# Four of a pair's seven block products in one PSUM bank

## The chip, the core and the metric

The kernel runs on one core of a Trainium2 chip. The metric is the time of one execution on the device, in microseconds. Its engines work side by side, each through its own instructions in order: TensorE (PE in the profile, its weight loads PEld), VectorE (DVE), ScalarE (ACT), GpSimd (POOL), and SyncE (SP), which here only issues transfers. TensorE writes its results to PSUM, eight banks of 128 x 512 float32 each; VectorE and ScalarE read them from there.

## The reference

The kernel computes one encoder block over 1024 tokens of width 1024: three attention mixers side by side, and a gate for each of them and each channel. What matters for this change are the gates. `mg` is the last part of one large projection of the normalised input, and gives 3 x 1024 gate channels per token:

```
h = rms_norm(x, g_pre)
..., mg = split(h @ w_in)
gates = sigmoid(mg + b_merge)            # 3 branches x 1024 channels
merged = gates[0] * ya + gates[1] * yb + gates[2] * ym
out = merged @ w_out
x = x + rms_norm(out, g_post)
```

Everything is float32. The kernel splits each operand of a product into a rounded high part and a remainder (low part) and adds three products: high x high, high x low, low x high.

## The kernel before, in words

The 24 groups of 128 gate channels are its units of work here. Two are computed elsewhere; the other 22 form 11 pairs. A pair's result is a matrix of 2 x 128 gate channels by 1024 tokens, over an inner width of 1024. The kernel computes it by Strassen's scheme in Winograd's form: weights and tokens are cut into 2 x 2 blocks, and seven block products take the place of eight. Each block product is 128 x 512 over an inner width of 512, twelve matmuls of 128 x 512 (four slices, three terms each). The token blocks (`TB`: B11, B21, B22 and the sums T1 to T4) are made once. The weight blocks are A11, A12 and A22 of a pair and its sums S1 to S4, listed with their partners in `PRODUCTS` (L1780).

The stage has its own PSUM pool with six banks (`phase_psum("ps_w", s1=6)`, L1767). The scheduler is off in it: TensorE, ScalarE, VectorE, GpSimd and SyncE each carry out their instructions in the order in which the program text issues them. The loop at L1937 goes over pairs `n` and products `i`, and does three things each time:

- `prod(n, i)` (L1801) issues the twelve matmuls of product `i` into a new bank.
- `evac(...)` (L1822) reads the product *before* this one out of its bank. A11 is copied to `p1` by ScalarE. A12 is added to `p1` by VectorE, multiplied with the row `rb` and returned to ScalarE as a gate result. S2 is added to `p1` into `v`, S3 to `v` into `y`, S4 to `v` into `w`, all by VectorE. A22 is added to `y`, S1 to `y` and to `w`; these give the other gate results. Each gate result is one addition, one multiplication (L1817, L1818), one tanh on ScalarE (L1819) and a 256 KB store from ScalarE's queue (L1820).
- `slot(n, i)` (L1882) prepares what comes later. `block_of` (L1791) splits a block: its high part by ScalarE (L105), its low part by VectorE (L106), into one of five buffers `ch`. `weight_sum` (L1786) makes S1 to S4 of the next pair on GpSimd (L1789), S2 from S1 and S4 from S2. `own_blocks` (L1697) splits A11 and A12 of the next pair at once. `load_pair` (L1693) loads 512 KB of weights on SyncE's queue; two buffers `wr` serve all pairs, so the second load of pair n+1 waits until A22, the last block taken from pair n's second load, has been split. The slots also carry other work: the last item of one attention mixer in pairs 0 to 5 (`com`: loads, weightings by VectorE at L1677, additions by GpSimd at L1679), and loads and gate products (`g_load`, `g_mult`, L1857) of the next stage in pairs 6 to 9.

What a slot hands back (`then`: tanh and store) is issued after the slot's work. In the last pair the order of products differs (`nth`, L1797): A22 comes before S4 and S1, and S1 goes to the other bank pool (`psd`), since the next stage opens a new pool over the six banks. That stage (`y_unit`, L1985) begins with products of the token tiles `hh` and `hl`; `g_split` (L1859) writes their new contents, the lower halves in slots 3 and 4 of the last pair, the upper halves, which hold T4 until A22 is done, in slots 5 and 6.

Of the kernel before, what the change touches and what calls it, by code (L numbers as in the profile page):

```python
# [10 lines left out]
AF = mybir.ActivationFunctionType  # L11
OP = mybir.AluOpType
# [38 lines left out]
def block(ctx: ExitStack, tc: tile.TileContext, x, xT, memT, cst, msk, bcst, tabA, gpost,  # L51
          wu, wv, wb, wmem, wbr, wout, out):
    nc = tc.nc
    V, A, G, PE = nc.vector, nc.scalar, nc.gpsimd, nc.tensor
# [7 lines left out]
    def psd():  # L62
        return ps.tile([P, 512], F32, name="d", tag="d", bufs=2)
# [15 lines left out]
    def pss1():  # L79
        return bank["p"].tile([P, 512], F32, name="s1", tag="s1", bufs=bank["n"][1])  # L80
# [16 lines left out]
    rb = const.tile([P, S], F32, name="rb")  # L97
# [6 lines left out]
    def split(dst_h, dst_l, src):  # L104
        A.activation(dst_h, src, AF.Copy)  # L105
        V.tensor_tensor(dst_l, src, dst_h.bitcast(F32), op=OP.subtract)  # L106
# [15 lines left out]
    def passes(out_ps, terms):  # L122
        n = len(terms)
        for i, (a, b) in enumerate(terms):
            PE.matmul(out_ps, a, b, start=i == 0, stop=i == n - 1)  # L125
# [119 lines left out]
    def pool(name, side="left"):  # L245
        p = tc.tile_pool(name=name, bufs=1, side=side, reuse_waits="tile")
        return p, p.__enter__()

    def close(p):
        p.__exit__(None, None, None)  # L250
# [209 lines left out]
    for k in range(8):  # L460
        if k % 2 == 0:
            load_wkv(k // 2)
        for e in range(2 if k == 0 else 1):
            t = slice(e * 512, e * 512 + 512) if k == 0 else slice(0, S)
# [29 lines left out]
    for c in range(2):  # L494
        t = st.tile([P, 4, 256], F32, name=f"mt{c}", tag=f"xk{c}")
# [215 lines left out]
    half = [slice(0, 512), slice(512, 1024)]  # L711
# [183 lines left out]
    lo, hi = half  # L895
    PRODUCTS = (("A11", "B11"), ("A12", "B21"), ("S2", "T2"), ("S3", "T3"), ("S4", "B22"), ("S1", "T1"), ("A22", "T4"))
# [6 lines left out]
    def slot():  # L903
        return vp.tile([P, 1024], R, name="sl", bufs=2)
# [264 lines left out]
    for n in range(28):  # L1169
        i, k = divmod(n, 4)  # L1170
# [17 lines left out]
        for stage in (2, 1, 0):  # L1188
            r, at = divmod(n - 6 - (0, 2, 3)[stage], 3)
# [26 lines left out]
    for n in range(28):  # L1216
        i, k = divmod(n, 4)
        an, bn = PRODUCTS[i]
# [4 lines left out]
        for j in range(4):  # L1223
            c = slice(j * 128, j * 128 + 128)
            for q, (a, b) in enumerate(((bh[:, c], wh_[:, k]), (bl[:, c], wh_[:, k]), (bh[:, c], wl_[:, k]))):
                PE.matmul(now[j // 2][:, half_cols[j % 2]], a, b, start=k == 0 and j % 2 == 0 and q == 0,  # L1226
                          stop=k == 3 and j % 2 == 1 and q == 2)
# [23 lines left out]
    for n in range(6):  # L1251
        for i, (an, bn) in enumerate(PRODUCTS):
            dst = pss1()
            ah, al = [z.rearrange("p (k f) -> p k f", k=4) for z in BK[n, an]]
            terms = []
# [47 lines left out]
    with tc.tile_pool(name="aa", bufs=1, reuse_waits="tile") as aa:  # L1303
# [387 lines left out]
        BL = {n: {} for n in range(len(pairs))}  # L1691

        def load_pair(n, u):  # L1693
            BL[n][u] = wp.tile([P, 1024], F32, name="wr", bufs=WR)
            nc.sync.dma_start(BL[n][u], wu[U_M + pairs[n][u]])

        def own_blocks(n):  # L1697
            wh = wp.tile([P, 1024], R, name="wh")
            wl = wp.tile([P, 1024], R, name="wl")
            split(wh, wl, BL[n][0])  # L1700
            for j in range(2):
                BL[n][("A11", "A12")[j]] = wh[:, half[j]], wl[:, half[j]]

        TB = {}
# [8 lines left out]
        def split_block(nm, k):  # L1713
            h, l = TB[nm][k]
            split(h, l, l.bitcast(F32))
# [26 lines left out]
        for n in range(len(seq)):  # L1742
# [5 lines left out]
            last = n + 1 == len(seq)  # L1748
# [24 lines left out]
    lo, hi = half  # L1773
# [6 lines left out]
    PRODUCTS = (("A11", "B11"), ("A12", "B21"), ("S2", "T2"), ("S3", "T3"), ("S4", "B22"), ("S1", "T1"), ("A22", "T4"))  # L1780
    last = len(pairs) - 1

    def part(n, j):
        return BL[n][j // 2][:, half[j % 2]]

    def weight_sum(n, j):  # L1786
        u, v, op = {1: (part(n, 2), part(n, 3), OP.add), 2: (SF[0], part(n, 0), OP.subtract),
                    3: (part(n, 0), part(n, 2), OP.subtract), 4: (part(n, 1), SF[1], OP.subtract)}[j]
        G.tensor_tensor(SF[j - 1], u, v, op=op)  # L1789

    def block_of(n, nm):  # L1791
        src = part(n, 3) if nm == "A22" else SF[int(nm[1]) - 1]
        t = sr.tile([P, 2, 512], R, name="ch", bufs=5)
        split(t[:, 0], t[:, 1], src)
        BL[n][nm] = t[:, 0], t[:, 1]

    def nth(n, i):  # L1797

        return PRODUCTS[{4: 6, 5: 4, 6: 5}.get(i, i) if n == last else i]

    def prod(n, i):  # L1801
        an, bn = nth(n, i)
        dst = psd() if (n, i) == (last, 6) else pss1()
        ah, al = [v.rearrange("p (k f) -> p k f", k=4) for v in BL[n][an]]
        passes(dst, [t for k in range(4) for t in (
            (ah[:, k], TB[bn][k][0]), (ah[:, k], TB[bn][k][1]), (al[:, k], TB[bn][k][0]))])
        return dst

    p1, v, y, w = [sr.tile([P, 512], F32, name=f"sp{j}") for j in range(4)]

    def add(dst, x, z):
        V.tensor_tensor(dst, x, z, op=OP.add)

    def gate_out(n, u, t, x, z):
        r = sr.tile([P, 512], F32, name="rs", bufs=4)
        j = pairs[n][u]
        add(r, x, z)  # L1817
        V.tensor_tensor(r, r, rb[:, half[t]], op=OP.mult)  # L1818
        return lambda: (A.activation(r, r, AF.Tanh, scale=0.5, bias=hbm[:, j:j + 1]),  # L1819
                        nc.scalar.dma_start(thd[j, :, half[t]], r))  # L1820

    def evac(n, i, ps_):  # L1822

        nm = nth(n, i)[0]
        if nm == "A11":
            A.activation(p1, ps_, AF.Copy)
        elif nm == "A12":
            return gate_out(n, 0, 0, ps_, p1)
        elif nm == "S2":
            add(v, ps_, p1)  # L1830
        elif nm == "S3":
            add(y, ps_, v)
        elif nm == "S4":
            add(w, ps_, v)
        elif nm == "A22":
            return gate_out(n, 1, 0, ps_, y)
        else:
            outs = gate_out(n, 1, 1, ps_, y), gate_out(n, 0, 1, ps_, w)
            return lambda: [f() for f in outs]
# [4 lines left out]
    def g_load(i, k):  # L1844
        ot = pre["p"].tile([P, S], F32, name="ot", bufs=4)
        nc.sync.dma_start(ot, od[i, k])
        GG[i, k] = [ot]
        if i == 1:
            return
        gt = my.tile([P, S], F32, name="raw", bufs=3) if i < 2 and k % 2 else pre["p"].tile([P, S], F32, name="gt", bufs=1)  # L1850
        nc.sync.dma_start(gt, g2d[i, k])
        GG[i, k].append(gt)
# [6 lines left out]
    def g_split(i, k, t):  # L1859
        b = k + 4 * (i == 0)  # L1860
        split(hh[b][:, t], hl[b][:, t], GG[i, k][0][:, t])
# [4 lines left out]
    def y_load(m):  # L1866
        if m < len(steps):
            _, i, f = steps[m]
            YW[m] = wp.tile([P, 1024], F32, name="wr", bufs=WR)
            nc.sync.dma_start(YW[m][:, 0:512], wbr[i, f])  # L1870
# [11 lines left out]
    def slot(n, i):  # L1882

        first = n == 0
        if not first and i == 1 and n < last:
            load_pair(n + 1, 1)
        if i == 6 and n + 1 < last:
            load_pair(n + 2, 0)
        todo_ = (("S2",), ("S3", "A22"), ("S4",), ("S1",)) if first else (("A22",), ("S4",), ("S1",))
        for nm in todo_[i] if i < len(todo_) else ():  # L1890
            block_of(n, nm)
        if first:
            for nm, k in {1: (("T1", 0), ("T1", 1)), 2: (("T1", 2), ("T1", 3)), 3: (("T4", 0), ("T4", 1), ("T4", 2), ("T4", 3))}.get(i, ()):
                split_block(nm, k)
        if n < last:
            if i == 3:
                weight_sum(n + 1, 1)
                weight_sum(n + 1, 3)
                own_blocks(n + 1)
            elif i == 4:  # L1900
                weight_sum(n + 1, 2)
                block_of(n + 1, "S3")
            elif i == 5:
                weight_sum(n + 1, 4)
                block_of(n + 1, "S2")
        if (n, i) in COM:
            com[COM[n, i]]()
        if (n, i) == (6, 0):
            close(cbp)
            pre["pp"], pre["p"] = pool("pre", "right")  # L1910
        k = n - (last - 4)
        if 0 <= k < 4:
            if i == 0:
                g_load(2, k)
            elif i == 4:
                g_mult(2, k)
        if n == last:
            if i == 0:
                y_load(0)
                y_load(1)  # L1920
            elif i in (3, 4):
                for k in range(2 * i - 6, 2 * i - 4):
                    g_split(2, k, lo)
            elif i in (5, 6):
                for k in range(2 * i - 10, 2 * i - 8):
                    g_split(2, k, hi)
            if i == 2:
                y_split(0)
                y_load(2)

    for j in (1, 2, 3, 4):
        weight_sum(0, j)
# [4 lines left out]
    for n in range(len(pairs)):  # L1937
        for i in range(7):
            ps_ = prod(n, i)
# [125 lines left out]
    ORDER = (("A11", "B11"), ("A12", "B21"), ("S2", "T2"), ("S1", "T1"), ("S4", "B22"), ("S3", "T3"), ("A22", "T4"))  # L2065
# [117 lines left out]
    q, r = ss[7], ss[7][:, 3:4]  # L2183
# [146 lines left out]
```

## Time and profile before

| what | value |
|---|---|
| time, median of 3 runs | 1414.94 us (1414.56 to 1415.76) |
| profiled execution, first to last instruction (span) | 1412.1 us |
| median of the runs over that span | 2.84 us |
| TensorE busy | 1389.9 us (98%) |
| VectorE busy | 1054.0 us (75%) |
| ScalarE busy | 665.0 us (47%) |
| GpSimd busy | 500.3 us (35%) |
| mean granted TensorE clock | 0.999 |

The profile is of one execution; its own time beyond the span is not listed, so its numbers are set against the span, and the last two rows of times say how the span stands to the runs. A row of an order in time reads: start in us, duration in us, engine and line of the program, operation, output<-inputs, shape, count, and in brackets the idle time ahead of it with the instruction that ended it. "x2" means two instructions run together into one row. Buffer numbers are left out of the names: `s` is a bank of the stage, `sp` one of p1, v, y, w, `rs` a gate result, `sf` a weight sum, `ch` a split block, `wr` loaded weights, `thd` the gate results in memory, `og` and `ot` attention and gate operands. "issue" rows of a queue (SPq, ACTq) are the issuing of a transfer, not the transfer.

### The profile page before, as it was taken

The numbers are of one execution on the slowest core, as the hardware profiler recorded it, in microseconds if no ns is written. First come the engines' busy times: TensorE is split into PE (matmuls) and PEld (weight loads), VectorE is DVE, ScalarE is ACT, GpSimd is POOL, SyncE is SP. The second block draws the span as 40 slices with busy tenths as digits, with TensorE's granted clock in tenths as the row PEclk, the third lists the DMA queues.
The fourth block names the chain that finished last, engine by engine and source line by source line (L and its number), as shares of the span: only waits on it lengthen the run. The fifth ranks groups of instructions, "written<-read, shape, count | busy, mean of one in ns | idle before, by whom it ended". The sixth has DMA issues, their size and how long they took to land.

```text
span 1412.1 us, 21576 instructions
## 1 busy us (share of the span) xinstructions
PE 1389.9 (98%) x7640; PEld 1126.2 (80%) x7640; DVE 1054.0 (75%) x1839; ACT 665.0 (47%) x1414; POOL 500.3 (35%) x390
## 2 busy tenths in 40 slices
PE   7999999999999999999999999999999999999997
PEld 7799986666666889888888878787888888888886
DVE  7768677767763688788875777765878788677977
ACT  6544365666555445222146666656443334222332
POOL 0416702666657000333153353520423331035303
PEclk9999999999999999999999999999999999999999
DMA  6356532322210787445643554555343543866255
GB/s 235 101 179 211 186 109 86 116 83 71 83 55 25 243 261 240 125 148 175 201 140 90 135 162 115 138 144 180 106 150 127 176 175 124 323 216 207 94 206 179
DMA packets 121852, 216.01 MB, mean 153 GB/s; under 512 B 25424, under 2 KB 58000, under 8 KB 121744
## 3 DMA queue, kind: packets, MB, share of 16 engines
q1 hardware_dynamic: 106096, 189.17, 42.0%
q10 hardware_dynamic: 15648, 25.47, 4.9%
q8 instruction: 60, 0.98, 0.3%
q14 instruction: 48, 0.39, 0.1%
HBM read 149.21 MB, written 65.37 MB: 152 GB/s over the span
## 4 chain that ended last, share of the span: by engine, by line
PE 88%; DVE 4%; ACT 3%; DMA 2%; POOL 2%; issue 1%; SPq 0%; DVEq 0%; ACTq 0%; POOLq 0%
PE s L125 23%; PE sc L125 9%; PE d L143 7%; PE d L147 6%; PE d L145 6%; PE s L1177 4%; PE s L2101 4%; PE ov L809 4%; PE s L1226 3%; PE tr L1522 3%; PE s L1466 3%; PE s L794 2%; PE s L793 2%; PE tr L775 2%; PE d L2101 2%; PE d L550 1%
## 5 line engine op out<-in xcount | busy, mean ns | idle before, releaser
L143 PE MATMUL d<-hh,wh 128*128 128x512 f32 x480 | 195.1, 406 | 2.4 <-DVE fth L228 2.4
L145 PE MATMUL d<-hl,wh 128*128 128x512 f32 x480 | 194.3, 405 | 0.0
L147 PE MATMUL d<-hh,wl 128*128 128x512 f32 x480 | 190.9, 398 | 0.0
L800 POOL TENSOR_TENSOR bl<-bl,bp 128x512 f32<-128x512 f32 x96 | 130.6, 1361 | 54.4 <-ACT bp L796 49.0
L105 ACT ACTIVATE wh<-wr 128x512 fp32r<-128x512 f32 (+1 forms) x93 | 72.5, 787 | 122.1 <-PE sc L125 75.3
L106 DVE TENSOR_TENSOR wl<-wr,wh 128x1024 fp32r<-128x1024 f32 (+1 forms) x67 | 85.3, 1285 | 50.2 <-ACT wh L105 50.2
L125 PE MATMUL sc<-hh,wh 128*128 128x512 f32 x384 | 118.5, 389 | 0.0
L143 PEld LDWEIGHTS d<-hh,wh 128*128 128x128 f32 x480 | 90.5, 188 | 27.8 <-issue 6.6
L147 PEld LDWEIGHTS d<-hh,wl 128*128 128x128 f32 x480 | 90.6, 189 | 21.0 <-issue 4.5
L1479 ACT ACTIVATE pra<-pra,sts 128x192 f32<-128x192 f32 (+2 forms) x192 | 84.3, 442 | 46.3 <-DVE sts L1478 45.8
L145 PEld LDWEIGHTS d<-hl,wh 128*128 128x128 f32 x480 | 90.6, 189 | 19.2 <-issue 4.5
L796 ACT ACTIVATE bp<-s 128x512 f32<-128x512 f32 x128 | 75.7, 595 | 43.3 <-PE s L794 42.3
L776 DVE TENSOR_REDUCE bn<-tr 128x1 f32<-128x512 f32 x128 | 84.9, 683 | 12.8 <-PE tr L775 11.7
L125 PEld LDWEIGHTS sc<-hh,wh 128*128 128x128 f32 x384 | 72.1, 188 | 14.9
L1330 DVE SCALAR_TENSOR_TENSOR t2a<-d,tab 32x512 f32<-32x512 f32 x96 | 65.9, 687 | 23.2 <-PE d L147 21.4
L2006 POOL TENSOR_TENSOR acc<-acc,th 128x1024 f32<-128x1024 f32 x15 | 41.4, 2757 | 109.1 <-DVE th L2005 109.1
L1789 POOL TENSOR_TENSOR sf<-wr 128x512 f32<-128x512 f32 x22 | 29.8, 1373 | 131.3 <-DVE ch L106 57.4
L125 PE MATMUL sc<-hl,wh 128*128 128x512 f32 x192 | 74.8, 389 | 0.0
L125 PE MATMUL s<-hh,ch 128*128 128x512 f32 x224 | 73.5, 390 | 0.0
L1334 POOL TENSOR_TENSOR aq<-t1a,t2a 128x512 f32<-128x512 f32 x24 | 44.6, 1861 | 72.0 <-DVE t1a L1333 72.0
L1819 ACT ACTIVATE rs<-rs,hbm 128x512 f32<-128x512 f32 x44 | 31.8, 722 | 76.5 <-DVE rs L1818 75.8
L1397 POOL TENSOR_TENSOR ak<-kraw,kswp 128x512 f32<-128x512 f32 x24 | 47.8, 2015 | 54.7 <-DMA std<-sr 21.2
(500 smaller groups left out, 3775.6 us busy)
## 6 DMA issues: line engine op xcount, KB each, us to landing
wr<-in_wu SPq DMA_DIRECT2D x64, 512.0 KB
th<-thd SPq DMA_DIRECT2D x24, 512.0 KB
thd<-rs ACTq DMA_DIRECT2D x44, 256.0 KB
kd<-vy ACTq DMA_DIRECT2D x32, 256.0 KB
g2d<-fth SPq DMA_DIRECT2D x24, 256.0 KB
wos<-os SPq DMA_DIRECT2D x12, 512.0 KB
kraw<-kd SPq DMA_DIRECT2D x12, 512.0 KB
kswp<-kd SPq DMA_DIRECT2D x48, 128.0 KB
```

What stands on the lines that cost most here:

```text
L105: A.activation(dst_h, src, AF.Copy)
L106: V.tensor_tensor(dst_l, src, dst_h.bitcast(F32), op=OP.subtract)
L125: PE.matmul(out_ps, a, b, start=i == 0, stop=i == n - 1)
L143: PE.matmul(dst, wh[:, k, :], hh[k][:, t], start=k == 0, stop=False)
L145: PE.matmul(dst, wh[:, k, :], hl[k][:, t], start=False, stop=False)
L147: PE.matmul(dst, wl[:, k, :], hh[k][:, t], start=False, stop=k == 7)
L776: fp["last"] = V.tensor_reduce(st[i]["n"][:, j, c:c + 1], s, axis=AX.X, op=OP.min)
L796: A.activation(pp, s, AF.Exp, scale=-1.0)
L800: G.tensor_tensor(lsum[i % 2], lsum[i % 2], pp, op=OP.add)
L1330: V.scalar_tensor_tensor(t2[i], p[j], -0.125, tab[1][j, t], op0=OP.mult, op1=OP.mult)
L1479: A.activation(src, src, AF.Exp, scale=-1.0, bias=bias, accum_out=sts[:, h, 1, T:T + 1])
L2101: PE.matmul(dst[:, e[0]:e[1]], a, b, start=k == 0 and q == 0, stop=k == 3 and q == 2)
```

## The change

Four products of a pair, A11, S2, S3 and A22, now go into one bank `XB[n]`: A11's first matmul starts the sum, and the other three add on to what is there. The bank so holds, one after another, the values that `p1`, `v`, `y` and A22's sum had. ScalarE copies the bank to `p1`, `v` and `y` after A11, S2 and S3; three additions per pair on VectorE go away, and A22 is multiplied straight from the bank. The order of products becomes A11, A12, S2, S4, S3, S1, A22, in the last pair too, so that another product lies between any two of the chain. TensorE waits ahead of S2, S3 and A22 until the copy of what the bank held is done.

The preparation moves with it. From the second pair on, slots 0, 1, 2 split S4, S1, A22 (before: A22, S4, S1). S3 of the next pair is split in slot 5, behind S2, in place of slot 4. The second load of the next pair goes out in slot 3 in place of slot 1. In the first pair, slots 1, 2, 3 split S4 and S3, then S1, then A22 (before: S3 and A22, S4, S1). In the last pair all four `g_split` of upper halves are in slot 6.

```diff
-    def nth(n, i):
-
-        return PRODUCTS[{4: 6, 5: 4, 6: 5}.get(i, i) if n == last else i]
+    CHAIN = ("A11", "S2", "S3", "A22")
+    ORDER = [PRODUCTS[i] for i in (0, 1, 2, 4, 3, 5, 6)]
+    XB = {}
 
     def prod(n, i):
-        an, bn = nth(n, i)
-        dst = psd() if (n, i) == (last, 6) else pss1()
-        ah, al = [v.rearrange("p (k f) -> p k f", k=4) for v in BL[n][an]]
-        passes(dst, [t for k in range(4) for t in (
-            (ah[:, k], TB[bn][k][0]), (ah[:, k], TB[bn][k][1]), (al[:, k], TB[bn][k][0]))])
+        an, bn = ORDER[i]
+        more = an in CHAIN[1:]
+        dst = XB[n] if more else psd() if n == last and an == "S1" else pss1()
+        if an == "A11":
+            XB[n] = dst
+        ah, al = [z.rearrange("p (k f) -> p k f", k=4) for z in BL[n][an]]
+        terms = [t for k in range(4) for t in (
+            (ah[:, k], TB[bn][k][0]), (ah[:, k], TB[bn][k][1]), (al[:, k], TB[bn][k][0]))]
+        for q, (a, b) in enumerate(terms):
+            PE.matmul(dst, a, b, start=q == 0 and not more, stop=q == 11, skip_group_check=an in CHAIN)
         return dst
...
-    def gate_out(n, u, t, x, z):
+    def gate_out(n, u, t, x, z=None):
         r = sr.tile([P, 512], F32, name="rs", bufs=4)
         j = pairs[n][u]
-        add(r, x, z)
-        V.tensor_tensor(r, r, rb[:, half[t]], op=OP.mult)
+        if z is not None:
+            add(r, x, z)
+        V.tensor_tensor(r, x if z is None else r, rb[:, half[t]], op=OP.mult)
...
         elif nm == "S2":
-            add(v, ps_, p1)
+            A.activation(v, ps_, AF.Copy)
         elif nm == "S3":
-            add(y, ps_, v)
+            A.activation(y, ps_, AF.Copy)
         elif nm == "S4":
             add(w, ps_, v)
         elif nm == "A22":
-            return gate_out(n, 1, 0, ps_, y)
+            return gate_out(n, 1, 0, ps_)
...
-        if not first and i == 1 and n < last:
+        if not first and i == 3 and n < last:
             load_pair(n + 1, 1)
         if i == 6 and n + 1 < last:
             load_pair(n + 2, 0)
-        todo_ = (("S2",), ("S3", "A22"), ("S4",), ("S1",)) if first else (("A22",), ("S4",), ("S1",))
+        todo_ = (("S2",), ("S4", "S3"), ("S1",), ("A22",)) if first else (("S4",), ("S1",), ("A22",))
...
             elif i == 4:
                 weight_sum(n + 1, 2)
-                block_of(n + 1, "S3")
             elif i == 5:
                 weight_sum(n + 1, 4)
                 block_of(n + 1, "S2")
+                block_of(n + 1, "S3")
...
-            elif i in (5, 6):
-                for k in range(2 * i - 10, 2 * i - 8):
-                    g_split(2, k, hi)
...
+            if i == 6:
+                for k in range(4):
+                    g_split(2, k, hi)
```

More of the change, by code (lines that the diff above doesn't have):

```diff
@@ L1822, in evac @@
     def evac(n, i, ps_):
-        nm = nth(n, i)[0]
+        nm = ORDER[i][0]
         if nm == "A11":
```

## The prediction

> **What bounds the kernel now.** I read the page's shares first, then the stretches of the stage in which the pairs run (from 987 us), then single instructions in order of time.
>
> ```profile
> span 1412.1 us, 21576 instructions
> PE 1389.9 (98%) x7640; PEld 1126.2 (80%) x7640; DVE 1054.0 (75%) x1839; ACT 665.0 (47%) x1414; POOL 500.3 (35%) x390
> ...
> 1006.00:1197.00 191.00, 191.00 (x845) 158.22 (x844) 154.55 (x199) 77.31 (x118) 61.35 (x38) 1.00 0.44 146
> ...
> 987.09 0.50 PE L125 MATMUL s<-hh,wh 128*128 128x512 f32 x1
> ...
> 1177.66 0.39 PE L125 MATMUL s<-hh,wh 128*128 128x512 f32 x1
> ...
> 1183.11 2.20 PE L125 MATMUL s<-wgt,ch 128*128 128x512 f32 x9
> ```
>
> In the stretch the columns are its length, then busy time (count) of PE, PEld, DVE, ACT, POOL, then clock, DMA share, GB/s. PE is busy through all of it, at full clock. From the first A11 (987.09) to that of pair 10 (1177.66) lie 70 products: 2.72 us each, 19.06 us a pair. No wait remains to be taken from PE, so work removed from VectorE (154.55 of 191 us) cannot shorten the stage by itself. The last row is the start of pair 10's S2, 5.45 us behind its A11.
>
> How far the evacuations run behind PE, the waits of PE do not tell: six banks hide it. The engines' own order does:
>
> ```profile
> 1146.95 0.60 ACT L1826 ACTIVATE sp<-s 128x512 f32<-128x512 f32 x1 [0.44 <-ACT rs L1819]
> ...
> 1162.25 0.72 ACT L1819 ACTIVATE rs<-rs,hbm 128x512 f32<-128x512 f32 x1 [0.60 <-DVE rs L1818]
> 1163.43 0.63 ACT L105 ACTIVATE ch<-wr 128x512 fp32r<-128x512 f32 x1 [0.46 <-ACT rs L1819]
> 1163.96 0.71 ACT L1819 ACTIVATE rs<-rs,hbm 128x512 f32<-128x512 f32 x1
> 1164.70 0.36 ACTq L1820 DMA_DIRECT2D thd<-rs  x1
> 1165.12 0.60 ACT L1826 ACTIVATE sp<-s 128x512 f32<-128x512 f32 x1 [0.44 <-ACT rs L1819]
> 1165.61 1.14 ACT L105 ACTIVATE ch<-sf 128x512 fp32r<-128x512 f32 x2
> ...
> 1183.50 0.60 ACT L1826 ACTIVATE sp<-s 128x512 f32<-128x512 f32 x1 [0.44 <-PE s L125]
> ```
>
> The copy of pair 10's A11 starts at 1183.50, after PE has begun S2 (1183.11). Today that is free. After the change S2 writes the bank that this copy reads, so PE must wait for it.
>
> **The change, part by part.** *Additions and copies.* Per pair VectorE loses three additions of 0.68 us (those into v and y, and A22's); ScalarE gains two copies of 0.60 us (as the row at 1165.12), 11 times each. Off PE's path both are worth nothing: 77.31 of 191 us on ScalarE leave room, and PE has no idle time to give back.
>
> *New waits on PE.* S2 waits for A11's copy, S3 for S2's, A22 for S3's, each with one product (2.72 us) in between. Behind the waiting matmul all of PE is queued. So what counts is how long ScalarE's order takes from one A11 copy to the next: as soon as that is over 19.06 us, the excess lands on PE every pair. Today it is 18.17 us (1146.95 to 1165.12) and 18.38 (to 1183.50).
>
> *The moved load.* A22's block is now split at slot 2 instead of 0, and the load of the next pair's second weights (load_pair(n+1,1), which takes A22's buffer) goes out at slot 3 instead of 1. POOL's sums need it, S2's and S3's blocks need the sums, and these two now sit together in slot 5, ahead of S1's evacuation on VectorE. This closes a loop through no PE work: copy of A11, A12's evacuation, A22's split, load, sums, S2/S3 splits, S1's evacuation, its tanh, S4's split, A22's tanh, next copy of A11. Its durations:
>
> ```profile
> 1164.81 0.33 SPq L1695 DMA_DIRECT2D wr<-in_wu  x1
> ...
> 1169.19 2.54 POOL L1789 TENSOR_TENSOR sf<-wr 128x512 f32<-128x512 f32 x2 [11.91 <-DMA wr<-in_wu]
> 1171.68 2.27 POOL L1789 TENSOR_TENSOR sf<-sf,wr 128x512 f32<-128x512 f32 x1
> ...
> 1117.94 1.30 POOL L1789 TENSOR_TENSOR sf<-sf,wr 128x512 f32<-128x512 f32 x1
> ...
> 1173.33 1.17 DVE L106 TENSOR_TENSOR ch<-sf,ch 128x512 fp32r<-128x512 f32 x1
> ...
> 1177.26 0.68 DVE L106 TENSOR_TENSOR ch<-sf,ch 128x512 fp32r<-128x512 f32 x1
> 1177.86 0.68 DVE L1812 TENSOR_TENSOR rs<-s,sp 128x512 f32<-128x512 f32 x1
> 1178.57 0.69 DVE L1818 TENSOR_TENSOR rs<-rs,rb 128x512 f32<-128x512 f32 x1
> 1179.18 0.68 DVE L1812 TENSOR_TENSOR rs<-s,sp 128x512 f32<-128x512 f32 x1
> ```
>
> A follower on another engine starts some 0.03 after its releaser; on the same engine I count start to start.
> - Copy to load issue: copy 0.49 (1165.12 to 1165.61), S1's high part 0.63, its low part 0.60 (1177.26 to 1177.86), A12's addition 0.71 (1177.86 to 1178.57), multiplication 0.61, A22's low part 0.69, two handovers 0.06: 3.79.
> - Load: 4.38 (1164.81 to 1169.19). A store was issued 0.11 before that load, as A12's will be beside the new one, so this is the nearest row.
> - Sums for S1 and S3 2.50, for S2 1.30, handover 0.03: 3.83.
> - S2's high part 0.66, its low part 1.10 (a row of 1.17, held up by POOL's fourth sum), S3's low part 0.60, then S1's addition, multiplication, addition, multiplication 0.71 + 0.61 + 0.71 + 0.69: 5.08.
> - Second tanh and its store 1.18 (1162.25 to 1163.43), S4's high part 0.53, A22's tanh and store 1.16 (1163.96 to 1165.12), handover 0.03: 2.90.
>
> That makes 19.98, or 0.92 over 19.06. Three pairs carry a weighting of the last attention item, four carry a gate product in the same queues:
>
> ```profile
> 1090.56 2.02 DVE L1677 TENSOR_TENSOR og<-og,wgt 128x1024 f32<-128x1024 f32 x1
> 1092.49 0.69 DVE L1812 TENSOR_TENSOR rs<-s,sp 128x512 f32<-128x512 f32 x1
> 1093.21 2.39 DVE L1818 TENSOR_TENSOR rs<-rs,rb 128x512 f32<-128x512 f32 x1
> ...
> 1092.66 2.40 POOL L1679 TENSOR_TENSOR og<-og 128x1024 f32<-128x1024 f32 x1 [9.95 <-DVE og L1677]
> ...
> 1174.43 2.31 DVE L1857 SCALAR_TENSOR_TENSOR ot<-ot,gt 128x1024 f32<-128x1024 f32 x1
> 1174.03 1.62 POOL L1789 TENSOR_TENSOR sf<-wr,sf 128x512 f32<-128x512 f32 x1
> ```
>
> The weighting stands between S1's split and A12's addition, inside the loop: +1.93 (1090.56 to 1092.49) in pairs 3, 4, 5. In 4 and 5 POOL's addition also stretches A12's multiplication from 0.69 to 2.39: +1.70 more. (Part of these two pairs' loss shows at S3, since S2's copy stands behind A12's tanh on ScalarE.) The gate product of pairs 6 to 9 comes, in slot 4, where the sums now start; the last two rows hold each other up (the product ends 1.09 after the sum does), so it costs the sums between 0 and 1.1: I take 0.55.
>
> *First pair.* The second load of pair 1 went out at once; it now waits for pair 0's A22 split, after S2's copy.
>
> ```profile
> 996.97 0.68 DVE L1812 TENSOR_TENSOR sp<-s,sp 128x512 f32<-128x512 f32 x1
> ```
>
> VectorE now comes to that split, of 0.69, where this addition stood, once S1's and T1's splits are done, and its high part on ScalarE stands behind S2's copy: an end between 997.7 (the row's place) and 999.1 (with that copy and the high part, 0.60 + 0.66, ahead of it). With the steps above (4.38, 3.83, 5.08, 2.90, copy 0.60) pair 1's copy ends at 1014.5 to 1015.9; S2 was due at 987.09 + 9 x 2.72 = 1011.6, so 2.9 to 4.3: I take 4.0, nearer the end where ScalarE sets it.
>
> *The end.* The four splits of the upper halves now all follow the last product (A22). They need 0.63 + 0.69 for the first and 0.60 for each more, while the next stage's first twelve matmuls (lower halves, 2.72) run: cost 0 with some 1 us to spare; with no such cover 3. The last S1 in the other bank pool keeps the handover of banks as it was: 0.
>
> **Sum.** 4.0 (first) + 2 x 0.92 (1 to 3) + 2.85 (3 to 4) + 2 x 4.55 (4 to 6) + 4 x 1.47 (6 to 10) = 23.7, all on PE in a stage that had no idle time. Against the profiled span: 1412.1 + 23.7 = 1435.8. The median of the runs shown, 1414.94, is 2.84 above that span, so 1438.7: I say 1439.
>
> *The load's price from both sides.* A load that shared the queues with two others took 6.30 (issue to the sum that waited):
>
> ```profile
> 1109.16 12.14 SPq L1695 DMA_DIRECT2D wr<-in_wu  x2
> ...
> 1115.46 2.53 POOL L1789 TENSOR_TENSOR sf<-wr 128x512 f32<-128x512 f32 x2 [12.69 <-DMA wr<-in_wu]
> ```
>
> At 6.30 the sum is some 41 (1456). Downwards the rows show no faster landing; below about 3.4 the plain pairs fall to PE's own 19.06, and the first pair, the weightings and gate products still leave 12 to 15 (1427 to 1430). I take 4.38, the nearest case.
> The Trainium skill (DMA: Bandwidth & Descriptors, section "Anatomy of one DMA — SWDGE (gpsimd) path") fits one DMA, on another issuing path, as 2.0 us plus bytes over 436 GB/s; for 512 KB an estimate from it is 3.2 us. By it the sum would be about 14 (1429). The row is 1.2 us longer, and the sum stays with the row.
>
> **The rivals.**
> 1. *The loop stays under PE's pace, no change.* If the load lands before POOL would be free anyway, the loop is today's 18.2 to 18.4 less about 2 us of additions, under 19.06, and the copies are on time: 1414.9. For it: today's loop. Against it: in pairs without extra work it decides from a landing of 3.4 us or less, and the weighting pairs would stall even then. 5 in 100.
> 2. *VectorE's relief counts, faster.* 33 additions of 0.68 are 22 us; if half of that were on the path, 1404. It decides only if PE had waits on VectorE, and 191.00 of 191.00 busy is against it. 3 in 100.
> 3. *The load is much cheaper in the loop, or the splits overlap better than laid out:* 12 to 15, so 1427 to 1430. 17 in 100.
> 4. *The clock falls after each stall.* After the idle start PE ran slow for 5.2 us:
>
> ```profile
> 6.75 0.58 PE L381 MATMUL s<-wbh,hh 128*128 128x256 f32 x1 [6.75 <-ACT hh L282]
> ...
> 11.54 0.41 PE L381 MATMUL ov<-wbh,hl 128*128 128x256 f32 x1
> 11.75 0.41 PE L381 MATMUL ov<-wbl,hh 128*128 128x256 f32 x1
> ...
> 12.37 0.28 PE L381 MATMUL s<-wbh,hh 128*128 128x256 f32 x1
> 12.49 0.28 PE L381 MATMUL s<-wbh,hl 128*128 128x256 f32 x1
> ...
> 53.55 0.51 PE L143 MATMUL d<-hh,wh 128*128 128x512 f32 x1 [2.39 <-DVE fth L228]
> 53.89 0.40 PE L145 MATMUL d<-hl,wh 128*128 128x512 f32 x1
> 54.13 0.40 PE L147 MATMUL d<-hh,wl 128*128 128x512 f32 x1
> ```
>
> Matmuls 0.21 apart there became 0.12 apart: some 2.2 us lost per such phase, 24 for eleven stalls, 1463. Against it: behind the idle 2.39 the spacing is 0.34 once and then 0.24, near the 0.227 of the stage (5.45 over 24 matmuls). Only the first stall (4.0) is longer; one phase there would add 2.2, inside my range. 7 in 100.
> The Trainium skill (TensorE: Matmul & The Clock Gate, section "A second HAM failure mode: psum-queue depth-cycling") tells of a kernel whose short idle gaps between bursts made the clock gate swing; it speaks for this rival, and the row at 53.55 against it.
>
> **How the numbers follow.** The forecast, a loop of 20 to 24 us that PE waits for, has 68 in 100; its own range, with landings of 4.0 to 4.93 and the estimates above, is 1431 to 1446. The range to 8 in 10 takes in rival 3 and landings up to 5.5: 1426 to 1452. Within 0.2% (2.8 us, about what runs that lie 1.2 us apart can tell) holds rival 1; faster is rival 2; all else is slower: 0.03, 0.05, 0.92.
>
> **What would show it.** Right: PE idle ahead of S2 in most pairs, ended by the ScalarE copy of A11, once some 4 us and then 1 to 2; idle ahead of S3 in pairs 4 and 5; starts of the A11 copies 20.0 apart in plain pairs and 23.6 in pairs 4 and 5; POOL's first sum waiting for the load in every pair; the stage some 24 longer and no other stage changed. Wrong: PE without waits there; waits that name the low part of a block; copies 19.06 apart; or matmuls spaced by much more than 0.23 behind a stall.

## The result, and the profile after

The changed kernel takes 1440.05 us (median of 5 runs, 1439.67 to 1441.93); the kernel before took 1414.94 beside it. The ratio is 1.0175 (95% interval 1.0163 to 1.0187): 25.1 us slower, against a forecast of 24 (1439).

The profiled execution of the kernel after was the longest of its runs, 1441.93 with a span of 1440.2. That of the kernel before was a short one: its span of 1412.1 lies 2.84 under the median, where time and span of one run differ by 1.7 to 1.8. So the spans differ by 28.1, and the rows show somewhat more loss than the medians. The first rows of its page:

```profile
span 1440.2 us, 21513 instructions
...
PE 1400.2 (97%) x7640; PEld 1129.7 (78%) x7640; DVE 1019.4 (71%) x1806; ACT 675.6 (47%) x1436; POOL 492.3 (34%) x390
```

VectorE has 33 instructions and 34.6 us of work less than before, ScalarE 22 instructions more; no gain from it shows in the time. The view by stretches of the kernel after, with the columns as in the prediction: first the stage, then what follows it.

```profile
985.00:1225.00 240.00, 222.19 (x954) 179.67 (x955) 136.36 (x183) 100.59 (x164) 62.62 (x45) 0.97 0.38 125
1225.00:1440.00 215.00, 207.32 (x923) 171.41 (x922) 163.72 (x190) 62.07 (x117) 54.41 (x37) 0.99 0.58 203
```

and of the kernel before, the 215 us behind the stage:

```profile
1197.00:1412.00 215.00, 207.31 (x924) 171.67 (x922) 163.52 (x189) 61.03 (x115) 54.55 (x37) 0.99 0.58 204
```

What follows is the same on PE (207.32 and 207.31 busy). The stage is where nearly all of the time went: from the first A11 to the next stage's first product it takes 235.94 in place of 209.61, 26.3 more. PE, busy throughout before, is now idle for 17.81 of 240 us, and the mean granted clock is 0.97. Another 1.56 of the 28.1 lies ahead of the stage, whose first A11 starts at 988.65 in place of 987.09. Nothing of the change stands there: in this execution the first matmul started 0.5 later, and matmuls were slow for a while behind a wait that ends at 53.45, where those of the kernel before (the row at 53.55 in the prediction) were not:

```profile
53.45 0.74 PE L143 MATMUL d<-hh,wh 128*128 128x512 f32 x1 [2.45 <-DVE fth L228]
53.99 0.63 PE L145 MATMUL d<-hl,wh 128*128 128x512 f32 x1
```

The waits of PE over the whole program, after (in total, times, longest):

```profile
PE s L1811 <- ACT sp L1832: 14.8, 9, 3.6
...
PE s L1811 <- ACT sp L1836: 2.7, 2, 2.2
```

L1832 is the copy of A11, L1836 that of S2. No row of before has such a wait. The order in time of the kernel after shows what the copies wait for; the rows are the copies of A11 and, for pairs 2 to 3, 3 to 4 and 9 to 10, the steps between two of them:

```profile
1016.35 0.60 ACT L1832 ACTIVATE sp<-s 128x512 f32<-128x512 f32 x1 [0.40 <-ACT rs L1825]
...
1038.03 0.60 ACT L1832 ACTIVATE sp<-s 128x512 f32<-128x512 f32 x1 [0.40 <-ACT rs L1825]
1041.83 9.73 SPq L1695 DMA_DIRECT2D wr<-in_wu  x2
1046.05 2.54 POOL L1789 TENSOR_TENSOR sf<-wr 128x512 f32<-128x512 f32 x2 [15.70 <-DMA wr<-in_wu]
1049.87 1.15 ACT L105 ACTIVATE ch<-sf 128x512 fp32r<-128x512 f32 x2 [1.98 <-POOL sf L1789]
1055.05 0.72 ACT L1825 ACTIVATE rs<-rs,hbm 128x512 f32<-128x512 f32 x1 [0.60 <-DVE rs L1824]
1057.83 0.60 ACT L1832 ACTIVATE sp<-s 128x512 f32<-128x512 f32 x1 [0.40 <-ACT rs L1825]
1063.55 11.21 SPq L1695 DMA_DIRECT2D wr<-in_wu  x2
1069.23 2.54 POOL L1789 TENSOR_TENSOR sf<-wr 128x512 f32<-128x512 f32 x2 [18.02 <-DMA wr<-in_wu]
1081.14 0.60 ACT L1832 ACTIVATE sp<-s 128x512 f32<-128x512 f32 x1 [0.40 <-ACT rs L1825]
...
1104.78 0.60 ACT L1832 ACTIVATE sp<-s 128x512 f32<-128x512 f32 x1 [0.40 <-ACT rs L1825]
1128.23 0.60 ACT L1832 ACTIVATE sp<-s 128x512 f32<-128x512 f32 x1 [0.43 <-ACT rs L1825]
...
1189.71 0.60 ACT L1832 ACTIVATE sp<-s 128x512 f32<-128x512 f32 x1 [0.40 <-ACT rs L1825]
1193.51 0.33 SPq L1695 DMA_DIRECT2D wr<-in_wu  x1
1197.83 3.14 POOL L1789 TENSOR_TENSOR sf<-wr 128x512 f32<-128x512 f32 x2 [14.74 <-DMA wr<-in_wu]
1202.25 1.15 ACT L105 ACTIVATE ch<-sf 128x512 fp32r<-128x512 f32 x2 [2.80 <-POOL sf L1789]
1207.44 0.72 ACT L1825 ACTIVATE rs<-rs,hbm 128x512 f32<-128x512 f32 x1 [0.60 <-DVE rs L1824]
1210.21 0.60 ACT L1832 ACTIVATE sp<-s 128x512 f32<-128x512 f32 x1 [0.40 <-ACT rs L1825]
```

Read the bracket of each copy: it did not wait for PE (before, the last copy did: the row at 1183.50 in the prediction) but for the tanh ahead of it on ScalarE. And read the bracket of POOL's sums: idle for 15 to 18 us until the load lands. Each step shown is released by the one above it, or by VectorE's work in between, all the way round. The plain pair takes 19.80 us (1038.03 to 1057.83), pairs 4 and 5 take 23.64 and 23.45, the last one 20.50; PE needs 19.06.

### The profile page after: what moved, and what is told of

Same layout as the page of the kernel before. It is cut to its first block, busy times and chain, and to the rows that moved or that the text cites. A ratio compares the mean times of both kernels' runs of the same rounds, so it can differ in the third digit from the quotient of the medians.

```text
span 1440.2 us, 21513 instructions
## 1 busy us (share of the span) xinstructions
PE 1400.2 (97%) x7640; PEld 1129.7 (78%) x7640; DVE 1019.4 (71%) x1806; ACT 675.6 (47%) x1436; POOL 492.3 (34%) x390
## 4 chain that ended last, share of the span: by engine, by line
PE 73%; DVE 8%; ACT 5%; POOL 5%; DMA 4%; issue 4%; ACTq 1%; SPq 0%; DVEq 0%; POOLq 0%
PE sc L125 9%; PE s L125 9%; PE d L143 6%; PE d L147 6%; PE d L145 6%; PE s L1177 4%; PE s L2107 4%; PE ov L809 3%; PE s L1226 3%; DMA wr<-in_wu 3%; POOL sf L1789 3%; PE s L1466 2%; PE tr L1522 2%; PE s L794 2%; PE s L793 2%
## 5 line engine op out<-in xcount | busy, mean ns | idle before, releaser
L106 DVE TENSOR_TENSOR wl<-wr,wh 128x1024 fp32r<-128x1024 f32 (+1 forms) x67 | 76.1, 1148 | 62.4 <-ACT wh L105 62.3
L143 PEld LDWEIGHTS d<-hh,wh 128*128 128x128 f32 x480 | 90.7, 189 | 28.1 <-issue 6.3
L106 DVE TENSOR_TENSOR ch<-sf,ch 128x512 fp32r<-128x512 f32 x44 | 34.6, 805 | 71.1 <-ACT ch L105 71.1
L1478 DVE CUSTOM_DVE_ANT_0 pra<-s,mask 128x192 f32<-128x192 f32 (+2 forms) x192 | 58.5, 347 | 10.1 <-PE s L1466 9.2
```

Source lines behind the costliest of these rows:

```text
L143: PE.matmul(dst, wh[:, k, :], hh[k][:, t], start=k == 0, stop=False)
```

## The experiments

The theory: the time is set by the loop that the moved A22 split and load close; the shared bank makes PE wait at S2 and S3. Rival explanations: the four products in one bank cost the time by themselves; the load is not on the path; the clock that falls behind a wait is the main cost. The first four kernels ran together (before 1415.35 there), the last three together (before 1414.66).

**The splits back, the bank kept.** From the second pair on, A22's block is split first again and the load goes out in slot 1; the bank shared by four products stays.

```diff
-        if not first and i == 3 and n < last:
+        if not first and i == 1 and n < last:
...
-        ... else (("S4",), ("S1",), ("A22",))
+        ... else (("A22",), ("S4",), ("S1",))
```

> The changed kernel with one thing put back from the second pair on: A22's block is split in slot 0 again (then S4, S1) and the second load follows in slot 1. One bank and the copies stay. Theory (the loop through the late load sets the time): copies of A11 fall back to 19.06 us apart, the stall at pair 1 stays (3.7 us and a slow phase of the clock of 2.9), about 2 us more in the pairs with weightings: 1420 to 1424. Rival (the copies between the four products cost the time, wherever the load is): no change from 1440.

Measured: 1423.68 us (1421.15 to 1425.27), ratio 1.0055 (1.0038 to 1.0071). The waits of PE in this kernel:

```profile
PE s L1811 <- ACT sp L1832: 3.6, 1, 3.6
...
PE s L1811 <- ACT sp L1836: 1.6, 2, 0.9
```

Of nine waits for A11's copy one is left, that of the first handover. Two thirds of the loss (25.1 us over the kernel before, now 8.3) go with the order of three splits and a load, while the bank is shared as before. So the shared bank alone does not cost them; splits and load were put back together, and this kernel does not tell their shares.

**The bank undone, the order kept.** S2, S3 and A22 get their own banks again with VectorE's additions; the order of products and all the preparation stay as in the kernel after.

```diff
-        more = an in CHAIN[1:]
+        more = False
...
-            A.activation(v, ps_, AF.Copy)
+            add(v, ps_, p1)
...
-            A.activation(y, ps_, AF.Copy)
+            add(y, ps_, v)
...
-            return gate_out(n, 1, 0, ps_)
+            return gate_out(n, 1, 0, ps_, y)
```

> The changed kernel's order and preparation with the one bank undone: S2, S3 and A22 go into banks of their own, and VectorE adds again as before; ScalarE's two new copies are gone. Theory: the loop of 20 to 24 us is still there without any wait for a copy; PE then waits for blocks made late (S4, S2) in place of copies: some 18 us above before, 1431 to 1436. Rival (the chain in one bank is the cost): the time of before, 1415.

Measured: 1435.86 us (1435.46 to 1436.68), ratio 1.0143 (1.0128 to 1.0158). The waits of PE:

```profile
PE s L1811 <- ACT ch L105: 8.9, 7, 2.5
```

Without the shared bank 20.5 of 25 us are still lost. PE no longer waits for a copy but for split blocks (`ch`): the loop is there all the same (A11's copies lie 19.87 to 20.08 apart in pairs without a weighting), and only the place at which PE meets it is another. What the shared bank adds to the late splits is some 4 us (the ratios 1.0175 and 1.0143 are each good to 0.0015 or so).

**The splits moved in the kernel before.** The reverse: the kernel before with nothing but the order of splits and the slot of the load changed.

```diff
-        if not first and i == 1 and n < last:
+        if not first and i == 3 and n < last:
...
-        ... else (("A22",), ("S4",), ("S1",))
+        ... else (("S4",), ("S1",), ("A22",))
```

> The kernel before with one thing taken from the change: from the second pair on slots 0, 1, 2 split S4, S1, A22 in place of A22, S4, S1, and the second load goes out in slot 3. Order of products, banks and additions as before. Theory: this alone makes the loop, laid out some 25 us above before: 1433 to 1442, with PE waiting for low parts of blocks (S2, A22). Rival (the chain in one bank is the cost): 1415.

Measured: 1443.89 us (1442.22 to 1444.89), ratio 1.0198 (1.0183 to 1.0213): as much as the whole change cost, and a little above the range expected. The waits of PE:

```profile
PE s L125 <- DVE ch L106: 9.7, 9, 2.3
...
PE s L125 <- ACT ch L105: 4.6, 4, 1.9
```

So this one step of the change, the late splits with the load behind them, suffices for its loss, with no bank shared and no copy awaited.

**The stalls filled.** After the change, the two longest waits, in pairs 1 and 4 ahead of S2, are followed by slow matmuls. The kernel after, in time order:

```profile
1017.00 4.21 PE L1811 MATMUL s<-wgt,ch 128*128 128x512 f32 x9 [3.55 <-ACT sp L1832]
1021.01 1.48 PE L1811 MATMUL s<-kraw,ch 128*128 128x512 f32 x3
...
1058.47 2.33 PE L1811 MATMUL s<-wgt,ch 128*128 128x512 f32 x9 [0.35 <-ACT sp L1832]
```

Nine matmuls take 4.21 us in the first row, 2.33 in the last. This kernel fills the two waits with twelve matmuls each whose result nobody reads:

```diff
+            if (n, i) in ((1, 2), (4, 2)):
+                idle = psd()
+                for q in range(12):
+                    PE.matmul(idle, BL[n]["A12"][0][:, 0:128], TB["B21"][0][0], start=q == 0, stop=q == 11)
```

> The changed kernel with twelve more matmuls of no use (2.7 us) ahead of S2 in pairs 1 and 4, into a bank nobody reads. Theory that the clock falls behind idle times over some 3 us: these two waits shrink from 3.6 and 3.2 us to under 1, the slow matmuls behind them (0.45 us apart for 5.3 us) go, and the time falls by about 2.8 us for each, to 1434 to 1435, though work is added. Rival (the slow matmuls come from something else, as the bank): 1440 or up to 5 us more.

Measured: 1440.96 us (1438.99 to 1442.56), ratio 1.0182 (1.0165 to 1.0199). The slow matmuls behind the two filled waits are gone from the profiled execution (matmuls behind another wait are slow instead, the row at 1110.46 in the last section):

```profile
1017.14 2.33 PE L1811 MATMUL s<-wgt,ch 128*128 128x512 f32 x9 [0.73 <-ACT sp L1832]
```

but the gain expected for it did not come. In the two profiled executions the stage is 3.1 us shorter here (first A11 to the next stage's first product, 232.80 against 235.94). Where slow matmuls were taken away, the handover from pair 1 to 2 gained: 19.83 in place of 21.68. That from 3 to 4 takes 22.21 in place of 23.31, but no slow matmuls lie in it in either kernel; its load landed sooner:

```profile
1061.88 0.33 SPq L1695 DMA_DIRECT2D wr<-in_wu  x1
1066.46 2.53 POOL L1789 TENSOR_TENSOR sf<-wr 128x512 f32<-128x512 f32 x2 [16.92 <-DMA wr<-in_wu]
```

That is 4.58 from issue to sum, and 5.68 in the kernel after (1063.55 to 1069.23). The second slow phase of the kernel after lies in the handover from 4 to 5, and that takes 23.49 here in place of 23.64: without slow matmuls PE comes to S3 earlier and waits there.

```profile
1086.97 0.96 PE L1811 MATMUL s<-kswp,ch 128*128 128x512 f32 x3 [1.85 <-ACT sp L1836]
```

The one profiled execution is the shortest of its runs and the other the longest, and the medians differ by 0.9 the other way, less than their intervals. The mean granted clock was 0.993 or 0.994 in each of the five runs of the kernel after, and 0.995 to 0.999 here; the run at 0.999 took 1440.85. So the expectation fell in size: a slow phase lets the next products come later, and where PE would have waited for the loop in any case, it costs next to nothing.

**The load made later.** The kernel after with the second load of each pair, from pair 2 on, issued twice, the second behind the first into the same buffer.

```diff
-            nc.sync.dma_start(BL[n][u], wu[U_M + pairs[n][u]])
+            for _ in range(2 if u == 1 and n > 1 else 1):
+                nc.sync.dma_start(BL[n][u], wu[U_M + pairs[n][u]])
```

> After's kernel; the second load of each pair from pair 2 on is issued twice, the second one into the same buffer behind the first, so that the same weights land about 4.3 us later; nothing else is computed differently. If the load stands in a closed loop that sets the pairs' pace (theory), each of the nine handovers from pair 1 on grows by about 4.2: the copies of A11 lie some 24 apart in plain pairs and 27 to 28 in pairs 4 and 5, and the time is about 1475 to 1483 (a little less where the load now has to wait less for others, up to 1500 if slow matmuls behind the longer waits add to it). If the load has slack and PE waits for something else (rival), the copies stay 20 to 23.6 apart and the time is 1440 to 1445.

Measured: 1470.44 us (1470.22 and 1470.67), ratio 1.0394 (1.0373 to 1.0415). In time order:

```profile
1213.78 0.60 ACT L1833 ACTIVATE sp<-s 128x512 f32<-128x512 f32 x1 [0.40 <-ACT rs L1826]
1217.57 4.41 SPq L1696 DMA_DIRECT2D wr<-in_wu  x2
1225.48 2.54 POOL L1790 TENSOR_TENSOR sf<-wr 128x512 f32<-128x512 f32 x2 [18.32 <-DMA wr<-in_wu]
...
1237.25 0.60 ACT L1833 ACTIVATE sp<-s 128x512 f32<-128x512 f32 x1 [0.40 <-ACT rs L1826]
```

From issue to sum it takes 7.91 (1217.57 to 1225.48), 3.59 more than the 4.32 of the kernel after in the same pair, not 4.2 as expected; the copies lie 23.47 apart, 2.97 more than 20.50. In this pair the gate product no longer runs beside the sums (2.54 in place of 3.14 for the first two), which gives back the other 0.6. Over the nine handovers concerned, the gaps between copies grew by 26.7 us: 1.6 from pair 1 to 2, where slow matmuls had already stretched the gap, and 2.9 to 3.5 in each other. Slow matmuls behind the last copy (4.31 us from S2 to S4 in pair 10, 2.85 in the kernel after, and 0.2 more up to S3) make it 28.4 of the 28.7 by which the span grew (1440.2 to 1468.9). A load that lands 3.59 later makes nearly every pair about 3 us longer, and that only a load on the closed path can do. The time lies 5 us under the range, by the size of the second landing.

**The first pair.** The first kernel of this section, and the first pair prepared in another order too:

```diff
-        todo_ = (("S2",), ("S4", "S3"), ("S1",), ("A22",)) if first ...
+        todo_ = (("S2",), ("S4", "A22"), ("S3",), ("S1",)) if first ...
```

> The kernel a22_first (chain kept, from pair 2 on A22's block split first and the next load back in slot 1), and the first pair gets the same: A22's block is split in slot 2 together with S4, S3's in slot 3. Theory: what was left of the loss, 8.3 us at the median, is the first pair's wait (3.6 and 1.7 of slow matmuls) and two waits at S3; the earlier split brings pair 1's copy of A11 forward by some 1.5 to 2.5 us, and pair 0's own A22 may wait about 1. Time 1419 to 1422, pair 1's wait ahead of S2 1 to 2.4 instead of 3.6. Rival (the rest is the price of four products in one bank, wherever blocks are split): 1423.7 as a22_first.

Measured: 1421.87 us (1420.21 to 1422.36), ratio 1.0052 (1.0035 to 1.0069), 7.2 us over the kernel before. In time order, pair 1's S2:

```profile
1015.50 2.33 PE L1811 MATMUL s<-wgt,ch 128*128 128x512 f32 x9 [2.60 <-ACT sp L1832]
```

The wait went from 3.59 to 2.60, where 1 to 2.4 was expected, and no slow matmuls follow. The time is within its range, but by ratio (1.0052 against 1.0055) it can't be told from the kernel without this step. In the profiled execution what is left adds up: 3.2 ahead of pair 1's S2 and 2.1 at S3 of pairs 4 and 5, with a little behind each, in a span (1418.4) 6.3 longer than that of the kernel before. All but 0.2 us of PE's waits that are left in the stage are for copies of the shared bank. So in this order of work the shared bank probably has a price of its own; a kernel with the early splits and a bank for each product was not run.

**The weightings moved too.** As the last, with the weightings of pairs 3, 4 and 5 in slot 4 instead of 1:

```diff
-    COM = {..., (3, 1): 4, (3, 2): 5, (4, 1): 6, (4, 2): 7, (5, 1): 8, (5, 6): 9}
+    COM = {..., (3, 4): 4, (3, 6): 5, (4, 4): 6, (4, 6): 7, (5, 4): 8, (5, 6): 9}
```

> As a22_first_all, and the weightings of the last attention item in pairs 3, 4, 5 move from slot 1 to slot 4, behind A12's gate result (their loads to slot 6). Theory: the waits at S3 of pairs 4 and 5 (0.8 and 1.1) came from the weighting ahead of A12's result and go; waits of up to 1 may come up elsewhere in the pair. Time 1417 to 1421. Rival: the weightings cost the same wherever they stand, so no difference to a22_first_all.

Measured: 1423.37 us (1421.87 to 1424.26), ratio 1.006 (1.0045 to 1.0075). The waits at S3 are gone, as the theory had it, and others have come at S2 of the next pairs. In time order:

```profile
1014.59 3.91 PE L1811 MATMUL s<-wgt,ch 128*128 128x512 f32 x9 [2.58 <-ACT sp L1832]
...
1093.30 2.34 PE L1811 MATMUL s<-wgt,ch 128*128 128x512 f32 x9 [0.64 <-ACT sp L1832]
1113.21 2.37 PE L1811 MATMUL s<-wgt,ch 128*128 128x512 f32 x9 [0.56 <-ACT sp L1832]
1133.70 1.65 PE L1811 MATMUL s<-wgt,ch 128*128 128x512 f32 x6 [1.12 <-ACT sp L1832]
```

The time is 2.4 over its range, and by the times the rival was right: a weighting of 2 us costs about the same in either place. The rest of the difference to the kernel above, in the profiled executions, are the slow matmuls behind pair 1's wait (the first row; S2 to S4 takes 4.45 there, 2.85 above; spans 1420.1 and 1418.4). No kernel tried here beats the one before; in this stage PE had no idle time that a better order could have given back.

## Why the prediction was right, point by point

**The loop.** Its five steps, predicted and measured in the plain pair 2 to 3 (rows of the kernel after above): copy to load 3.79, measured 3.80 (1038.03 to 1041.83); load 4.38, 4.22 (to 1046.05); sums 3.83, 3.82 (to 1049.87); splits and S1's two gate results 5.08, 5.18 (to 1055.05); tanh, split, tanh 2.90, 2.78 (to 1057.83). Together 19.98 and 19.80. Between plain pairs the kernel with filled stalls has 19.83 twice. That these steps set the pace was argued before; the late splits and load alone (1443.89), the load made later (1470.44) and splits and load put back (1423.68) show it.

**Rivals 1 to 3.** With plain pairs at 19.80 the loop is over PE's 19.06, not under it (rival 1); no wait of PE in the stage went away, since there was none (rival 2); the load takes 4.20 to 4.59 in eight of the nine handovers and 5.68 in the other, never 3.4 or less (rival 3). The prediction's sum of 41 for a landing of 6.30 leaves the first pair's 4.0 as it is, though a load is one of its steps; with it the sum is 42.9. So does its estimate of about 14, which then is 12.4. The range holds either way.

**Gate products.** Predicted 20.5 for pairs 6 to 10, measured 20.49 to 20.50. The sums took 4.42 in place of 3.82 (1197.83 to 1202.25), 0.60 more, with 0.55 taken.

**Weightings.** Pairs 4 and 5: 23.6 predicted, 23.64 and 23.45 measured. From pair 3 to 4 it was 23.31 and not 21.9: the weighting's 1.92 is there (copy to load 5.72 in place of 3.80), but the load took 5.68 (1063.55 to 1069.23), not 4.38. This is the one term of the loop that was mis-sized, by 1.30; its value lies between the two rows that the prediction had as bounds, 4.38 and 6.30. Two attention loads go out 1.9 ahead of it. What makes it long stays open: with the same two as far ahead it took 4.58 with the stalls filled, 5.14 with the splits moved in the kernel before and 5.43 with the bank undone. The waits at S3 came in pairs 3 (0.53) and 5 (2.22), where 4 and 5 were forecast; in pair 4 slow matmuls took the place of one, as the filled stalls show (1.85).

**First pair.** 4.0 predicted; by the start of S2, pair 0 to 1, PE lost 3.69 (22.75 between 994.25 and 1017.00, less 19.06), of which 3.55 is the wait.

**The clock (rival 4).** It was in part true: the two longest waits, 3.55 and 3.17, were each followed by some 5 us of half-rate matmuls, the nine others in the stage, up to 2.22, by none. Of each phase, 12 matmuls (S2 to S4) took 5.29 in place of 2.85 (pair 10). In the profiled execution the handover from pair 1 to 2 took 21.68 for it and not 20.0. But the price the prediction gave this rival, 2.2 per phase on top of the waits, is not what the filled stalls show: the phase in pair 1 cost 1.85, that in pair 4 0.15, since it fell into time that PE would have waited. And the row held against this rival, full pace behind an idle 2.39, was weak evidence: at the same place slow matmuls followed 2.45 in the kernel after (the row at 53.45).

**The sum.** By the starts of S2 the profiled execution lost 3.69, 2.87, 0.48, 4.26, 4.58 and 4.39 in the first six handovers, 5.74 in the next four and 0.1 behind the last; another 0.2 comes in because a pair took 19.04 and not 19.06 in the kernel before, counted by S2. Together that is 26.3, as the stage grew (209.61 to 235.94), against 23.7 predicted. The gap is pair 1's slow phase (1.9) and the long load of pair 3 (1.3), less what the first and the plain pair stayed under (0.3 and 0.4). The median run lost 25.1. That this is within 1.1 of the forecast is partly luck: the slow phase was not in the sum, and that one load differs by as much from kernel to kernel.

**What was costed at nothing.** The additions taken from VectorE gave no gain that shows: the kernel that has them back, in banks of their own, is 4 us faster than the one without, though bank and additions changed together there and are not told apart. The splits all at the end cost next to nothing: from pair 10's S2 to the next stage's first product it takes 13.73 (1210.86 to 1224.59), against 13.59 before (1183.11 to 1196.70).

## What to carry to other kernels

Where PE is busy without a gap, look for its limit in the order of the other engines: follow one buffer from the instruction that frees it, through the load that fills it, back to the instruction that frees it again, and add up the steps. If that comes near PE's time for one round, moving one 0.69 us split two places later, and a load with it, can cost more than all the additions that a change takes away. To tell a loop from a single late transfer, make one of its steps later by a known amount and see whether every round grows by that amount.

## What the runs showed of the hardware

How long PE must wait for slow matmuls to follow is not sharp. In the stage, in the kernels shown here, every single wait of 3.17 to 5.66 us was followed by them, and none of up to 1.88; between 1.97 and 2.6 both occur. At the same place, 2.60 was not (nine matmuls in 2.33, the row at 1015.50) and 2.58 was (3.91, the row at 1014.59). The shortest single one that was, 1.97, is in pair 9 of the kernel before with the splits moved; there three matmuls take 1.48 that take 0.84 in pair 10:

```profile
1186.04 2.20 PE L125 MATMUL s<-wgt,ch 128*128 128x512 f32 x7 [1.97 <-DVE ch L106]
1188.04 1.48 PE L125 MATMUL s<-kraw,ch 128*128 128x512 f32 x3
```

Two short waits with two matmuls between them were followed by slow ones too, in pair 5 of that kernel; the last seven of the product take 3.14 there, 1.88 in pair 10:

```profile
1096.83 0.73 PE L125 MATMUL s<-wgt,ch 128*128 128x512 f32 x2 [0.69 <-ACT ch L105]
1098.40 3.14 PE L125 MATMUL s<-wgt,ch 128*128 128x512 f32 x7 [0.84 <-DVE ch L106]
```

Three matmuls behind the wait for S2's copy in pair 5, in the kernel after:

```profile
1113.39 0.96 PE L1811 MATMUL s<-kswp,ch 128*128 128x512 f32 x3 [2.22 <-ACT sp L1836]
```

and in the kernel with filled stalls:

```profile
1110.46 1.65 PE L1811 MATMUL s<-kswp,ch 128*128 128x512 f32 x3 [2.21 <-ACT sp L1836]
```

The Trainium skill (TensorE: Matmul & The Clock Gate, section "HAM oscillation — how this bites in real kernels") has the clock fall behind gaps of more than about 3.4 us. The runs agree for the waits of 3.50 us and more, and show slow matmuls from 1.97 us on, though not each time.

An instruction of VectorE or POOL can hold up one that the other begins meanwhile: two sums on POOL took 2.54 alone and 3.14 when a gate product of VectorE had begun 0.47 before them (pair 9), and A12's multiplication on VectorE took 2.36 in place of 0.69 when an addition of POOL, of 2.37, had begun 0.55 before it (pair 4).
